# FoX attention on one core: splitting fp32 value products over two column tiles by query blocks instead of by even and odd key blocks

## The chip, the cores and the metric

The kernel runs on one core of a Trainium2 chip. The core has five engines with queues of their own: TensorE (PE), VectorE (DVE), ScalarE (ACT), GpSimd (POOL) and SyncE (SP), which issues most of the DMAs. The metric is the device time of one execution in microseconds. Of each kernel one further execution was profiled; all durations come from its trace.

## What is computed

One inference step of a small hybrid decoder: a recurrent layer (RG-LRU), then a forgetting-attention layer, for a prompt of 2048 tokens and for 8 sequences of 8 new tokens each that attend to 4096 cached tokens in pages. The change is in the attention of the prompt, which has 16 heads of 64 elements:

```python
def fox_block(q, k, v, cq, ck, q_pos, k_pos):
    s = jnp.einsum('bqhd,bkhd->bhqk', q, k).astype(jnp.float32) * (HEAD_DIM ** -0.5)
    s = s + jnp.swapaxes(cq, 1, 2)[:, :, :, None] - jnp.swapaxes(ck, 1, 2)[:, :, None, :]
    mask = k_pos[None, :] <= q_pos[:, None]
    s = jnp.where(mask[None, None], s, -jnp.inf)
    p = jax.nn.softmax(s, axis=-1)
    return jnp.einsum('bhqk,bkhd->bqhd', p.astype(v.dtype), v)
```

The last line is the value product: for each head, the weights `p` (keys by queries) times the values `v` (keys by 64). Everything is float32.

## The kernel before

**Stages.** The recurrent layer comes first, in two parts of the prompt; then the projections that make keys, values, queries and gates (`phase_b`, with streamed weights); then the prompt's attention (`attention`), and at the end the output projection (`project`). The decode of the 8 sequences (`decode`) reads 16 turns of cache pages by DMA, transposes the keys on DVE (`ktr`), makes scores on PE (`dS`) and value products on PE (`dO`). Two of its turns run earlier, the other fourteen beside the projections and the attention: `Side.along` takes steps of the decode in proportion to a cost that each step of the attention yields. The order of instructions on each engine is then set when the program is built, by a scheduler that works with a model of the engines; on the chip every engine runs its list in order.

**Units.** Attention works through 64 units, a head and a block of 512 queries each (`units`); even heads take the query blocks 0, 1, 2, 3 and odd heads 3, 2, 1, 0. A unit of query block `qc` has 4 x (`qc` + 1) blocks of 128 keys, so there are 640 key blocks in all. The last four key blocks of a unit are on the diagonal: the fourth sees only the last 128 queries, and `lo` is the first query that a key block needs (0, 128, 256, 384).

**One key block.** PE makes scores into an `st` bank (lines 1538 and 1539, on the diagonal also a causal mask, line 1541), ACT takes the exponential into `p` (line 1547), or into `acc` for the first key block of a unit. After every fourth key block a group of value products is recorded, to run two key blocks later (`product`). POOL then adds each `p` to `acc` (line 105, a helper), which gives the sums of the softmax. There are five `p` buffers and five `acc` buffers, two `st` banks, and one bank `ops` for the value products. Ahead of this, PE also makes the scores for the row maxima of later units (`sx`, line 1405), which DVE reduces.

**The value product.** The stationary operand is the values of 128 keys, 128 x 64; the moving operand is `p`, 128 x up to 512. An output has 64 rows, half of the array's columns. Even key blocks write rows 0 to 63 of `ops`, odd ones rows 64 to 127 (`r = k % 2 * HD`, line 1557), so two neighbouring products use two column tiles of the array. A group of four key blocks is held together in PE's order by `together`; it waits for the last of its four exponentials.

**The end of a unit** (`finish`). The two halves of `ops` are partial sums of the same output, over even and odd keys. ACT copies the upper rows to `oT` (line 1439) and the lower rows to `odd` (line 1443), and POOL adds `odd` to `oT` (line 105). Then come the sums' reduction (`total`), the normalisation (`norm`) and the gate, which reads `oT`.

The functions that the change touches:

Of the kernel before, what the change touches and what calls it, by code (L numbers as in the profile page):

```python
# [11 lines left out]
F32 = mybir.dt.float32  # L12
# [3 lines left out]
ALU = mybir.AluOpType  # L16
# [4 lines left out]
P = 128  # L21
# [7 lines left out]
HD = 64  # L29
# [15 lines left out]

SHARE = 1.13
LEAD = 18
ODD = "G"
RAMP = 8
NS = 3  # L50
SHARE0 = 2.0
# [33 lines left out]
def tile_hawk_fox(  # L85
# [8 lines left out]
    V, A, G, T, S = nc.vector, nc.scalar, nc.gpsimd, nc.tensor, nc.sync  # L94
# [9 lines left out]
    def tt(eng, out, a, b, op):  # L104
        eng.tensor_tensor(out, a, b, op=op)  # L105

    def together(mms, after=()):

        first = mms[0]().ins
        for d in after:  # L110
            tc.add_manual_dep(first, d.ins.name, SYNC)
        with tc.high_priority(), tc.issue_after(first):
            for mm in mms[1:]:
                mm()
# [91 lines left out]
    def sbuf(es, name, side=None):  # L206
        return es.enter_context(tc.tile_pool(name=name, bufs=1, side=side, reuse_waits="tile"))
# [1100 lines left out]
    def attention(es):  # L1308
        pool = sbuf(es, "att")
        ps3 = psum["att"]  # L1310

        ps3.tile([P, 512], F32, name="ops", tag="ops", bufs=1)
        ps3.tile([P, 512], F32, name="st", tag="st", bufs=2)
        pool.tile([P, 512], F32, name="acc", tag="acc", bufs=NACC)
        pool.tile([P, 512], F32, name="p", tag="p", bufs=NP)
# [3 lines left out]
        vvs = [pool.tile([P, 16, HD], F32, name=f"vvt{i}") for i in range(2)]  # L1319
# [38 lines left out]
        heads, qas, mxs, oTs_, sgt = {}, {}, {}, {}, {}  # L1358
# [10 lines left out]
        def load_keys(h):  # L1369
            kb = kbs[h % 2]  # L1370
            loaded.add(h)
            for lo, hi in halves(h):
                queue[0].dma_start(f(kb[0:64, lo:hi]), kd_d[h * HD:(h + 1) * HD, 1, lo:hi])
                queue[0].dma_start(f(kb[64:67, lo:hi]), nc_d[h, :, lo:hi])
# [14 lines left out]
        def load_low(u):  # L1389
            if u < len(units):  # L1390
                h, qc = units[u]
                qa = qas[u] = pool.tile([P, 512], F32R, name="qa", tag="qa", bufs=4)
                queue[0].dma_start(f(qa[:, :]), qd_d[h * HD:(h + 1) * HD, :, qc * 512:(qc + 1) * 512].rearrange("d x t -> (d x) t"))
# [36 lines left out]
        def finish(u, ops, acc):  # L1430
            h, qc = units[u]
            pr, h2 = divmod(h, 2)
            if u % 8 == 0:
                oTs_["sums"] = pool.tile([P, 32], F32, name="sums", tag="sums", bufs=2)
            sums = oTs_["sums"]
            if h2 == 0:
                oTs_[qc] = pool.tile([P, 512], F32, name="oT", tag="oT", bufs=5)
            oT = oTs_[qc][h2 * HD:(h2 + 1) * HD, :]
            A.copy(oT, ops[0:HD, :])
            lo = P if qc == 0 else 0  # L1440
            if ODD == "G":
                odd = pool.tile([P, 512], F32, name="odd", tag="odd")[h2 * HD:(h2 + 1) * HD, :]
                A.copy(odd[:, lo:], ops[HD:, lo:])
                tt(G, oT[:, lo:], oT[:, lo:], odd[:, lo:], ALU.add)
            else:
                tt(V, oT[:, lo:], oT[:, lo:], ops[HD:, lo:], ALU.add)
            accs.append((qc, acc))
            if len(accs) == 4 or h == H - 1:
                later.after(2, lambda todo=accs[:]: total(h2, sums, todo, h >= H - 2))
                accs.clear()  # L1450
            if u >= len(units) - 4:
                later.after(5, lambda oT=[oTs_[qc]]: norm(pr, sums, qc, 1, oT))
            elif u % 8 == 7:
                later.after(5, lambda oT=[oTs_[c] for c in range(4)]: norm(pr, sums, 0, 4, oT))
# [45 lines left out]
        start = [sum(nks[:u]) for u in range(len(units))]  # L1500
# [27 lines left out]
        ops = acc = None  # L1528
        pair = []
        for u, (h, qc) in enumerate(units):  # L1530
            load_low(u + 2)
            for k in range(nks[u]):
                ka, kb = heads[h], kbs[h % 2]
                qa, qb = qas[u], qbs[u % NQ]
                lo = max(0, k - qc * 4) * P
                ks = slice(k * P, (k + 1) * P)
                ps = ps3.tile([P, 512], F32, name="st", tag="st", bufs=2)
                T.matmul(ps[:, lo:], ka[:, ks], qa[:, lo:], start=True, stop=False)  # L1538
                T.matmul(ps[:, lo:], kb[:, ks], qb[:, lo:], start=False, stop=(k < qc * 4))  # L1539
                if k >= qc * 4:  # L1540
                    T.matmul(ps[:, lo:lo + P], identB[:, :], causal[:, :], start=False, stop=True)
                done[2] = u + (k == nks[u] - 1)
                if k == 0:
                    p = acc = pool.tile([P, 512], F32, name="acc", tag="acc", bufs=NACC)
                else:
                    p = pool.tile([P, 512], F32, name="p", tag="p", bufs=NP)
                pair.append((k, lo, p, A.activation(p[:, lo:], ps[:, lo:], AF.Exp)))  # L1547

                def product(u=u, h=h, todo=pair, acc=acc, last=(k == nks[u] - 1)):


                    nonlocal ops
                    if todo[0][0] == 0:
                        ops = ps3.tile([P, 512], F32, name="ops", tag="ops", bufs=1)

                    def mm(k, lo, p, _):
                        r = k % 2 * HD
                        return T.matmul(ops[r:r + HD, lo:], vvs[h % 2][:, k, :], p[:, lo:], start=(k < 2),  # L1558
                                        stop=(last and k >= todo[-1][0] - 1))

                    together([partial(mm, *x) for x in todo], [todo[-1][3]])
                    for k, lo, p, _ in todo:
                        if k:
                            tt(a_l(), acc[:, lo:], acc[:, lo:], p[:, lo:], ALU.add)
                    if last:
                        finish(u, ops, acc)

                if k % 4 == 3:
                    later.after(2, product)
                    pair = []  # L1570
                before = done[0]
                advance(tick)
                tick += 1
                later.tick()
                if k + sum(nks[u - u % 4:u]) == 0 and h + 1 < H:
                    load_keys(h + 1)
                if k + sum(nks[u - u % 4:u]) == 3 and h + 1 < H:
                    load_head(h + 1)
                yield 4.1 * (512 - lo) * 0.42 + (done[0] - before) * 213
# [130 lines left out]
    todo = a00.norm(2)  # L1710
# [35 lines left out]
    todo = a01.norm(3)  # L1746
# [40 lines left out]
    dec, att, last = ExitStack(), ExitStack(), ExitStack()  # L1787
# [11 lines left out]
    lin.close()  # L1799
    psum["att"] = banks(att, "psa", 6)  # L1800
    side.along(attention(att), share)
    side.upto(1e12)
    project(last)
# [37 lines left out]
```

## Time and profile before

| | |
|---|---|
| median of three runs | 3070.52 us (3066.45, 3070.52, 3083.66) |
| the profiled execution | 3073.57 us, span of its instructions 3071.8 us |
| busy over the span | PE 2826.8 us (92%), DVE 1805.2 (59%), ACT 1294.9 (42%), POOL 1158.7 (38%) |
| first and last value product | 1739.5 us, 2898.0 us |
| value products | 1152 records from `p` and 128 from `acc` |

A row of a group reads: line, engine, operation, output and inputs with their shapes, count; then total busy time in us and the mean of one in ns; then the idle time of that engine just before, and what ended it. A row of the timeline reads: start in us, duration in us, engine, line, operation, count; in brackets the idle time before it. A row of waits reads: who waited for whom, us in total, how often, the longest. A piece of the chain of work that ended last reads: start, duration, engine, tile and line. PE is the matmul, PEld the load of its stationary operand. An fp32 matmul of the program is two records in the trace. In a PE row, `128*64 128x512` is an operand of 128 rows for a tile of 64 columns, and 512 moving columns.

### The profile page before, as it was taken

To read this page: it belongs to the slowest core of one execution; us is meant where nothing else is said; L and a number is where in the kernel's file an instruction comes from. 1 tells how busy PE (TensorE), PEld (TensorE's weight loads), DVE (VectorE), ACT (ScalarE), POOL (GpSimd) and SP (SyncE) were. 2 spreads that over 40 slices of the span, in tenths; PEclk is the share of its full clock that TensorE was granted. 3 is DMA by queue.
4 is the path that set the end of the run, shared out by engine and by line. 5 is a ranking of instruction groups with operands and counts; after the bars stand their busy time and mean duration, and the time that the engine had idled before them with its cause. 6 is when DMAs were issued, how large, how long until landed. Compare 5 with 4: busy or idle time off the path is not lost.

```text
span 3071.8 us, 58144 instructions
## 1 busy us (share of the span) xinstructions
PE 2826.8 (92%) x20462; PEld 2178.9 (71%) x20462; DVE 1805.2 (59%) x4012; ACT 1294.9 (42%) x2874; POOL 1158.7 (38%) x1263
## 2 busy tenths in 40 slices
PE   5998999999999989997999798998989989999898
PEld 5997889988999978896888454555545554554587
DVE  7876555424357756755555566666667765543244
ACT  4665432222346655333333244343434445455321
POOL 1653201000025532000000365656565757788522
PEclk9999999999999999998999799999999999999999
DMA  4224547788622256999999998989999997322243
GB/s 121 91 76 147 157 137 209 239 256 260 209 82 86 86 180 202 318 312 313 329 311 316 303 285 258 293 276 306 294 309 316 328 286 236 107 67 68 83 143 111
DMA packets 492855, 653.25 MB, mean 213 GB/s; under 512 B 91100, under 2 KB 292829, under 8 KB 485286
## 3 DMA queue, kind: packets, MB, share of 16 engines
q1 hardware_dynamic: 488934, 643.87, 66.8%
q10 hardware_dynamic: 3340, 3.56, 0.4%
q8 instruction: 162, 2.65, 0.4%
q0 software_dynamic: 288, 2.10, 0.2%
q14 instruction: 131, 1.07, 0.1%
HBM read 513.82 MB, written 135.16 MB: 211 GB/s over the span
## 4 chain that ended last, share of the span: by engine, by line
PE 56%; DMA 18%; DVE 10%; ACT 6%; SPq 5%; issue 4%; POOL 2%; DVEq 0%; ACTq 0%; POOLq 0%
PE ops L1558 6%; DMA raw<-in_cache_k_dram 4%; PE y L367 4%; PE y L368 4%; PE y L369 4%; PE st L1538 4%; DMA raw<-in_cache_v_dram 4%; PE sx L1405 3%; PE kv L369 3%; PE kv L367 3%; PE kv L368 3%; PE dO L1236 3%; PE st L1539 3%; PE dS L1126 2%; PE qg L367 2%
## 5 line engine op out<-in xcount | busy, mean ns | idle before, releaser
L105 POOL TENSOR_TENSOR acc<-acc,p 128x512 f32<-128x512 f32 (+3 forms) x576 | 640.6, 1112 | 304.6 <-PE ops L1558 240.8
L1547 ACT ACTIVATE p<-st 128x512 f32<-128x512 f32 (+3 forms) x576 | 290.5, 525 | 409.5 <-PE st L1539 186.6
L1158 DVE STREAM_TRANSPOSE ktr<-raw 128x1024 f32<-128x1024 f32 x256 | 305.3, 1224 | 151.2 <-DMA raw<-in_cache_k_dram 141.8
L1407 DVE TENSOR_REDUCE mxs<-sx 128x1 f32<-128x512 f32 x384 | 253.6, 679 | 145.0 <-PE sx L1405 144.2
L368 PE MATMUL kv<-wl,xh 128*128 128x256 f32 (+3 forms) x1088 | 309.9, 288 | 9.0 <-DVE wl L412 8.8
L367 PE MATMUL kv<-wh,xh 128*128 128x256 f32 (+3 forms) x1088 | 311.0, 290 | 5.8 <-ACT wh L411 5.7
L369 PE MATMUL kv<-wh,xl 128*128 128x256 f32 (+3 forms) x1088 | 310.1, 287 | 0.0
L1558 PE MATMUL ops<-p,vvt 128*64 128x512 f32 (+3 forms) x1152 | 296.9, 554 | 2.3 <-ACT p L1547 2.1
L1538 PE MATMUL st<-qa,ka 128*128 128x512 f32 (+3 forms) x640 | 273.6, 428 | 21.1 <-ACT p L1547 16.6
L1405 PE MATMUL sx<-kbt,qbt 96*128 96x512 f32 (+3 forms) x640 | 232.3, 421 | 26.3 <-DMA qbt<-qd 10.6
L1538 PEld LDWEIGHTS st<-qa,ka 128*128 128x128 f32 x640 | 124.1, 194 | 179.5 <-issue 112.9
L411 ACT ACTIVATE wh<-wst,gv 128x256 fp32r<-128x256 f32 (+1 forms) x384 | 164.4, 499 | 187.7 <-DMA wst<-in_b_w_in_dram 73.2
L1539 PE MATMUL st<-qbt,kbt 128*128 128x512 f32 (+3 forms) x640 | 236.5, 371 | 0.0
L412 DVE SCALAR_TENSOR_TENSOR wl<-wst,gv,wh 128x256 fp32r<-128x256 f32 (+1 forms) x384 | 170.4, 494 | 104.6 <-ACT wh L411 100.8
L367 PE MATMUL qg<-xh,wh 128*128 128x384 f32 (+2 forms) x640 | 228.8, 359 | 0.0
L369 PE MATMUL qg<-xh,wl 128*128 128x384 f32 (+2 forms) x640 | 227.6, 357 | 1.1 <-DVE wl L412 1.0
L368 PE MATMUL qg<-xl,wh 128*128 128x512 f32 (+2 forms) x640 | 227.0, 356 | 0.0
L1091 POOL TENSOR_TENSOR qw<-qb,amask 128x128 f32<-128x128 f32 x64 | 29.8, 473 | 502.7 <-PE dS L1126 354.0
L368 PEld LDWEIGHTS kv<-wl,xh 128*128 128x128 f32 (+1 forms) x1088 | 204.3, 189 | 12.7 <-DVE wl L412 10.4
L367 PEld LDWEIGHTS kv<-wh,xh 128*128 128x128 f32 (+1 forms) x1088 | 204.3, 189 | 12.2 <-ACT wh L411 6.5
L369 PEld LDWEIGHTS kv<-wh,xl 128*128 128x128 f32 (+1 forms) x1088 | 206.0, 190 | 4.4 <-issue 4.3
L1405 PEld LDWEIGHTS sx<-kbt,qbt 96*128 96x128 f32 x640 | 117.6, 201 | 93.7 <-issue 31.1
(299 smaller groups left out, 6477.2 us busy)
## 6 DMA issues: line engine op xcount, KB each, us to landing
raw<-in_cache_k_dram SPq DMA_DIRECT2D x512, 256.0 KB
raw<-in_cache_v_dram SPq DMA_DIRECT2D x512, 256.0 KB
wst<-in_w_kv_dram SPq DMA_DIRECT2D x48, 512.0 KB
wst<-in_b_w_in_dram SPq DMA_DIRECT2D x48, 512.0 KB
xt<-in_x_prompt_dram SPq DMA_DIRECT2D x32, 512.0 KB
wst<-in_a_w_in_dram SPq DMA_DIRECT2D x64, 256.0 KB
out_dram<-kf SPq DMA_DIRECT2D x128, 128.0 KB
sc<-cd SPq DMA_DIRECT2D x16, 1024.0 KB
```

The costliest lines, as they stand in the source:

```text
L105: eng.tensor_tensor(out, a, b, op=op)
L367: T.matmul(ps, lh(k), rh(k), start=(k == 0), stop=False)
L368: T.matmul(ps, lh(k), rl(k), start=False, stop=False)
L369: T.matmul(ps, ll(k), rh(k), start=False, stop=(k == nk - 1))
L412: V.scalar_tensor_tensor(wl[:, k, :], st[:, k, :], gk, f(wh[:, k, :]), op0=ALU.mult, op1=ALU.subtract)
L1158: V.transpose(t.kts[pp][:, n], raw[:, :, pp * 256:(pp + 1) * 256])
L1405: T.matmul(ps[:, :w], qb[0:96, j * P:(j + 1) * P], kb[0:96, ck * 512:ck * 512 + w], start=True, stop=True)
L1407: V.reduce_max(mx[:, j, ck:ck + 1], ps[:, :w], axis=AX.X)
L1538: T.matmul(ps[:, lo:], ka[:, ks], qa[:, lo:], start=True, stop=False)
L1539: T.matmul(ps[:, lo:], kb[:, ks], qb[:, lo:], start=False, stop=(k < qc * 4))
L1547: pair.append((k, lo, p, A.activation(p[:, lo:], ps[:, lo:], AF.Exp)))
L1558: return T.matmul(ops[r:r + HD, lo:], vvs[h % 2][:, k, :], p[:, lo:], start=(k < 2), stop=(last and k >= todo[-1][0] - 1))
```

## The change

Each key block now has two value products instead of one, with the same stationary operand: query blocks 0 and 2 of the unit go to the first column tile, query blocks 1 and 3 to the second (`r` = 0, 1). Each product is at most 256 wide and reads `p` with a step. The output of a unit is then 128 x 256, complete in both halves, and takes half a bank; units take the two halves of one bank in turn. At a unit's end ACT makes two copies of 64 x 256 straight into the places of `oT`; `odd` and POOL's add are gone. A diagonal key block has products only where a query block needs it: a group on the diagonal has seven products, a full group eight, where both had four.

```diff
-ODD = "G"
...
-        ps3.tile([P, 512], F32, name="ops", tag="ops", bufs=1)
+        ops2 = ps3.tile([P, 512], F32, name="ops", tag="ops", bufs=1)
...
-            oT = oTs_[qc][h2 * HD:(h2 + 1) * HD, :]
-            A.copy(oT, ops[0:HD, :])
-            lo = P if qc == 0 else 0
-            if ODD == "G":
-                odd = pool.tile([P, 512], F32, name="odd", tag="odd")[h2 * HD:(h2 + 1) * HD, :]
-                A.copy(odd[:, lo:], ops[HD:, lo:])
-                tt(G, oT[:, lo:], oT[:, lo:], odd[:, lo:], ALU.add)
-            else:
-                tt(V, oT[:, lo:], oT[:, lo:], ops[HD:, lo:], ALU.add)
+            oT = oTs_[qc][h2 * HD:(h2 + 1) * HD, :].rearrange("d (a r c) -> d a r c", a=2, r=2)
+            for r in range(2):
+                A.copy(oT[:, :, r, :], ops[r * HD:(r + 1) * HD, :].rearrange("d (a c) -> d a c", a=2))
...
                     if todo[0][0] == 0:
-                        ops = ps3.tile([P, 512], F32, name="ops", tag="ops", bufs=1)
-
-                    def mm(k, lo, p, _):
-                        r = k % 2 * HD
-                        return T.matmul(ops[r:r + HD, lo:], vvs[h % 2][:, k, :], p[:, lo:], start=(k < 2),
-                                        stop=(last and k >= todo[-1][0] - 1))
-
-                    together([partial(mm, *x) for x in todo], [todo[-1][3]])
+                        ops = ops2[:, u % 2 * 256:u % 2 * 256 + 256]
+
+                    def mm(k, lo, p, r):
+                        a0 = (lo // P + 1 - r) // 2
+                        return T.matmul(ops[r * HD:(r + 1) * HD, a0 * P:], vvs[h % 2][:, k, :],
+                                        p[:, :].rearrange("p (a r c) -> p a r c", a=2, r=2)[:, a0:, r, :],
+                                        start=(k == 0), stop=(last and k == todo[-1][0] - 1 + r))
+
+                    together([partial(mm, k, lo, p, r) for k, lo, p, _ in todo for r in range(2) if lo <= (2 + r) * P],
+                             [todo[-1][3]])
```

Up to the first value product the order of instructions is the same on every engine. From there on it differs, since the scheduler places the new instructions. In the changed kernel lines up to 1308 are numbered one lower, and the products have line 1551 instead of 1558. On PE, at the first two groups of value products (the diagonal of unit 0, then the first group of unit 1), before:

```order
8757 L1558 MATMUL ops<-acc,vvt_19534 64x512
8758 L1558 MATMUL ops<-p,vvt_19534 64x384
8759 L1558 MATMUL ops<-p,vvt_19534 64x256
8760 L1558 MATMUL ops<-p,vvt_19534 64x128
8761 L1538 MATMUL st<-qa,ka 128x512
...
8773 L1541 MATMUL st<-causal,identB 128x128
8774 L1558 MATMUL ops<-acc,vvt_19534 64x512
8775 L1558 MATMUL ops<-p,vvt_19534 64x512 x3
```

And in the changed kernel, where `x6` counts equal neighbours:

```order
8757 L1551 MATMUL ops<-acc,vvt_19534 64x256 x2
8758 L1551 MATMUL ops<-p,vvt_19534 64x128
8759 L1551 MATMUL ops<-p,vvt_19534 64x256
8760 L1551 MATMUL ops<-p,vvt_19534 64x128 x3
8761 L1531 MATMUL st<-qa,ka 128x512
...
8773 L1404 MATMUL sx<-kbt_19537,qbt_19541 128x512 x2
8774 L1551 MATMUL ops<-acc,vvt_19534 64x256 x2
8775 L1551 MATMUL ops<-p,vvt_19534 64x256 x6
```

The diagonal group went from four products to seven and the full one from four to eight, at the same places. On POOL, from the sums of unit 0 to those of unit 2 (`qw` and `gmx` belong to the decode), before:

```order
461 L105 TENSOR_TENSOR acc<-acc,p 128x384
462 L105 TENSOR_TENSOR acc<-acc,p 128x256
463 L105 TENSOR_TENSOR oT<-oT,odd 64x384
464 L105 TENSOR_TENSOR acc<-acc,p 128x128
465 L105 TENSOR_TENSOR acc<-acc,p 128x512 x3
466 L1091 TENSOR_TENSOR qw<-qb,amask 128x128
467 L105 TENSOR_TENSOR acc<-acc,p 128x512
```

And in the changed kernel:

```order
461 L104 TENSOR_TENSOR acc<-acc,p 128x384
462 L104 TENSOR_TENSOR acc<-acc,p 128x256
463 L104 TENSOR_TENSOR acc<-acc,p 128x128
464 L104 TENSOR_TENSOR acc<-acc,p 128x512 x4
465 L1090 TENSOR_TENSOR qw<-qb,amask 128x128 x2
```

The add of `odd` stood in front of an add to `acc` and is gone. On PE, where the decode's key scores (`dS`) stand beside the first groups of the fourth unit, before:

```order
8872 L1558 MATMUL ops<-acc,vvt_19534 64x512
8873 L1558 MATMUL ops<-p,vvt_19534 64x512 x3
8874 L1538 MATMUL st<-qa,ka 128x512
8875 L1539 MATMUL st<-qbt_19541,kbt_19537 128x512
8876 L1126 MATMUL dS<-ktr,qw 32x128 x32
8877 L1405 MATMUL sx<-kbt_19545,qbt_19542 128x512 x3
...
8885 L1558 MATMUL ops<-p,vvt_19534 64x512 x4
```

And in the changed kernel:

```order
8871 L1551 MATMUL ops<-acc,vvt_19534 64x256 x2
8872 L1551 MATMUL ops<-p,vvt_19534 64x256 x6
8873 L1531 MATMUL st<-qa,ka 128x512
8874 L1532 MATMUL st<-qbt_19541,kbt_19537 128x512
8875 L1203 MATMUL dsum<-ddg,ones 128x64
...
8884 L1551 MATMUL ops<-p,vvt_19534 64x256 x8
...
8898 L1125 MATMUL dS<-ktr,qw 32x128 x32
```

One group of key scores now stands behind the second group of value products of this unit instead of behind the first; by the 240th key block both orders have issued 1536 of these matmuls.

## The prediction

> **What bounds the kernel now.** The order of instructions is the same in both kernels until the first value product of the prompt's attention, so I first read the busy time of each engine in the three stretches that can differ: attention beside the decode, attention after the decode has ended, and the output projection.
>
> ```profile
> span 3071.8 us, 58144 instructions
> core 0: us, PE busy (x) PEld busy (x) DVE busy (x) ACT busy (x) POOL busy (x), PEclk, DMA share, GB/s
> 1740.00:2580.00 840.00, 775.10 (x6778) 441.13 (x6775) 565.12 (x1156) 371.04 (x900) 524.50 (x505) 0.96 0.94 295
> 2580.00:2898.00 318.00, 293.41 (x1265) 156.73 (x1264) 136.45 (x318) 162.50 (x340) 242.25 (x210) 0.97 0.33 88
> 2898.00:3072.00 174.00, 158.98 (x678) 127.95 (x676) 76.00 (x243) 33.98 (x77) 44.58 (x36) 0.96 0.39 127
> ```
>
> For 840 us two resources are full together: PE is busy for 92% of the time and the DMA engines for 94%, on the cache pages of the decode. In the next 318 us only PE is full (293.4 us, 24.6 us idle); POOL is at 76% and ACT at 51%. The last stretch holds no value product but the end of the very last one, and I leave it as it is. Next, the chain of work that ended last, by line, in the first and in the second stretch:
>
> ```profile
> by line: PE ops L1558 14.8%; PE st L1538 8.9%; PE sx L1405 7.3%; DMA raw<-in_cache_v_dram 7.3%; PE dO L1236 7.3%; DMA raw<-in_cache_k_dram 6.9%; PE st L1539 6.0%; PE dS L1126 5.8%; issue 4.4%; SPq L1073 3.7%; DMA rawn<-ksd 2.5%; DVE ktr L11
> by line: PE ops L1558 22.9%; PE st L1538 12.4%; PE sx L1405 8.6%; PE st L1539 8.2%; issue 4.0%; ACT p L1547 3.8%; PE y L367 3.6%; PE y L369 3.5%; PE y L368 3.5%; PE tot L1461 3.4%; DMA wst<-in_b_w_out_dram 3.1%; DMA ogd<-sgt 2.3%; SPq L466
> ```
>
> The value products themselves (`ops`) are the largest item of both: 14.8% of 840 us and 22.9% of 318 us, 124 + 73 = 197 us. So two questions decide: does a value product get dearer on PE, and how much of what ACT and POOL are spared stands on the chain?
>
> **PE: twice the products at half the width.** This is one group of four key blocks in the trace of before, in time order (start, duration, engine), with the first load of what follows it; then a diagonal group, and two groups of the decode that use narrower column tiles, and the loads of both kinds over the whole run:
>
> ```profile
> 2408.80 0.20 PEld L1558 LDWEIGHTS ops<-p,vvt 128*64 128x64 f32 x4 [0.36 <-ACT p L1547]
> 2408.81 1.94 PE L1558 MATMUL ops<-p,vvt 128*64 128x512 f32 x8
> 2409.29 0.14 PEld L1558 LDWEIGHTS ops<-p,vvt 128*64 128x64 f32 x2 [0.29 <-issue]
> 2409.72 0.14 PEld L1558 LDWEIGHTS ops<-p,vvt 128*64 128x64 f32 x2 [0.29 <-issue]
> ...
> 2420.29 1.50 PE L1558 MATMUL ops<-p,vvt 128*64 128x512 f32 x8
> ...
> 2405.43 1.07 PE L1236 MATMUL dO<-raw,sx 128*32 128x256 f32 x16
> ...
> 2422.73 1.96 PE L1126 MATMUL dS<-ktr,qw 128*32 128x128 f32 x64
> ...
> L1558 PEld LDWEIGHTS ops<-p,vvt x1152: 132/137/232, 1739.5 to 2897.8; 128*64 128x64 f32 x192
> ...
> L1126 PEld LDWEIGHTS dS<-ktr,qw x4096: 106/110/178, 579.4 to 2508.7; 128*32 128x32 f32 x196
> ```
>
> Each fp32 product is two records, so four products are eight. The loads of a pair come 0.43 us apart (2409.29, 2409.72): two records, one in each column tile, run side by side. Per tile the full group is four records of 512 columns, the `dO` group (four column tiles) four of 256, and the `dS` group sixteen of 128. With a start a, a charge c per record and s per column: a + 4c + 1024s = 1.07, a + 4c + 2048s = 1.94, a + 16c + 2048s = 1.96. The first two give s = 0.85 ns a column, the last two 12c = 0.02 us, c = 1.7 ns. So sixteen narrow records cost what four wide ones do.
>
> After the change a full group has, per tile, eight records of 256 columns: the same 2048 columns, four more charges, 1.94 + 0.007 us. In a diagonal group the longer tile had 2 x (512 + 256) = 1536 columns (even blocks) and then has 2 x (256 + 256 + 128 + 128) = 1536 (odd query blocks): also only four charges. There are 640 / 4 = 160 groups, so PE gains 160 x 0.007 = 1.1 us of work; the chain carried 197 us of the (96 x 1.94 + 64 x 1.50) = 282 us that these groups take, 70%, so +0.8 us. From below: nothing makes the streaming shorter, so no gain; from above, the second and third rival.
>
> The Trainium skill speaks against the change here: "TensorEngine Tiling (Array Packing)", section Instruction Overhead, gives each matmul about 60 cycles of overhead; at the 2.4 GHz of "TensorE: Matmul & The Clock Gate" that is, as an estimate, 25 ns, so four more records in each of 160 groups would cost 16 us of PE and the sum below would end some 11 us later. The `dS` row does not agree: at 25 ns its twelve additional records a tile would show 0.3 us, and it shows 0.02.
>
> **ACT and POOL at the end of a unit.** Here are the copies and the add that the change replaces, the two rows nearest to the new copy (256 elements a partition), and what was waited for:
>
> ```profile
> L1439 ACT COPY oT<-ops 64x512 f32<-64x512 f32 x64 | 37.1, 579 | 107.4 <-PE ops L1558 107.3
> L1443 ACT COPY odd<-ops 64x512 f32<-64x512 f32 (+1 forms) x64 | 35.6, 556 | 0.9
> L105 POOL TENSOR_TENSOR oT<-oT,odd 64x512 f32<-64x512 f32 (+1 forms) x64 | 77.3, 1208 | 88.2 <-ACT odd L1443 85.2 <-issue 2.3
> L1547 ACT ACTIVATE p<-st 128x256 f32<-128x256 f32 x63 | 24.0, 381 | 23.0 <-PE st L1541 13.9 <-POOL acc L105 8.5
> L1260 ACT COPY ob<-dO 128x256 f32<-128x256 f32 x11 | 4.1, 371 | 17.1 <-PE dO L1244 17.0
> ACT p L1547 <- POOL acc L105: 34.9, 34, 3.6
> ACT p L1547 <- POOL acc L105: 17.9, 18, 3.4
> ```
>
> Two copies of 0.579 and 0.556 become two of about 0.375 (the copy's own row says 371, the exponential's 381): 0.385 us a unit, 64 x 0.385 = 24.6 us of ACT. POOL loses 64 adds, 77.3 us, and the wait in front of them (85.2 us for the `odd` copy) in which later `acc` adds stood behind it in POOL's queue. Those adds free the five `p` buffers, and ACT waited for them 34.9 us in all, 17.9 of it in the second stretch. Little of this is on the chain, though. It has 7 pieces of the first copy (7 x 0.58), 8 of the second (2.86 us in all, five of them near full length), 3 of the add and 7 of `acc` adds (5.4 us in all); first and last of each, and all of the add:
>
> ```profile
> 1866.36 0.58 ACT oT L1439
> 1866.95 0.59 ACT odd L1443
> 1884.66 1.28 POOL oT L105
> 1893.01 1.01 POOL oT L105
> ...
> 1891.11 1.02 POOL acc L105
> ...
> 2820.45 0.58 ACT oT L1439
> 2821.04 0.59 ACT odd L1443
> 2821.70 1.27 POOL oT L105
> 2822.97 0.42 POOL acc L105
> ```
>
> First copies: 7 x 0.205 = -1.4 us. The five long second copies: 2.70 - 5 x 0.375 = -0.8. The add: -3.6. Of the `acc` pieces five stand right behind an add of `oT` (3.7 us); half of that, -1.8, because the product they wait for is late next. With PE's +0.8 the sum is -6.8 us. Ends: 0 if PE or a cache page is late at the same moment anyway, and the whole idle time of PE in the second stretch, 24.6 us, as the first rival has it.
>
> What costs nothing. The half banks: the first product of the next unit starts behind its own four exponentials, and ACT, in order, has made the copies before those in both kernels, so the single bank was no wait and two halves free none. The last unit's shorter end lies beside the projection. `odd` leaves SBUF, which nothing asks for. SP's own instructions are unchanged; their places move a little (fourth rival).
>
> The profiled execution took 3073.57 us (span 3071.8), 3.05 over the median of 3070.52. Against its own time the sum gives 3066.8, against the median 3063.7: **3064 us**.
>
> **Rivals.**
>
> 1. *The queues drain better than the chain shows*: 3047 us. The chain names only the last of several late things. In the second stretch nothing but PE is full; ACT's 17.9 us behind POOL and 19 units x 0.385 = 7.3 us of copies add up to 25.2, just what would fill PE's 24.6 us of idle time. 3070.5 - 24.6 + 0.8. For it: POOL at 76% there, with units whose adds come in runs. Against: much of that idle time is the turn-round from score to exponential to product.
>
> 2. *A charge for every record*: 3082 us. The first two records of a group that I looked at stand 0.48 us apart from their successors and the later ones 0.43 to 0.44:
>
> ```profile
> 2402.90 0.64 PE L1558 MATMUL ops<-acc,vvt 128*64 128x512 f32 x1
> ...
> 2403.38 0.59 PE L1558 MATMUL ops<-acc,vvt 128*64 128x512 f32 x1
> ```
>
> If that 0.04 us were due for each record and not once a group: 4 x 160 x 0.04 x 0.70 = 18 us on 3064. At the price that the Trainium skill gives under Instruction Overhead it would be 3075. Against both: the `dS` row.
>
> 3. *Loads no longer hidden*: 3121 us, the slower side. A load of 64 columns takes 137 ns; a record of 256 columns streams for 0.218 us, so the two tiles' loads hide only while they overlap. Taken in turn they need 0.274: +0.056 x 8 = 0.45 us in a full group, and in a diagonal one 14 x 0.137 - 1.31 = 0.61. 96 x 0.45 + 64 x 0.61 = 82 us, 70% on the chain, 57. It decides once a load in turn exceeds 0.109 us. For it: loads double. Against: `dS` hides four loads of 110 ns behind every 0.11 us.
>
> 4. *The decode moves*: 3086 us. PE's order places a group of key scores later near the fourth unit. There are 38 of them (x2432 records of 64) in the first stretch, one each 22 us; if the pages behind it come one group late and the DMA engines, 94% full, never make it up, +22 us.
>
> ```profile
> L1126 PE MATMUL dS<-ktr,qw 128*32 128x128 f32 x2432 | 80.1, 287 | 5.5 <-DVE ktr L1158 3.4 <-issue 1.0 <-DVE oTs L105 0.9
> ```
>
> Against: 6% of 840 us is 50 us of slack, and by mid-stretch the decode stands level in both orders.
>
> **How the numbers follow.** Forecast 0.50; rivals 0.22, 0.08, 0.07, 0.13. Three runs of before lie 17 us apart, and a difference of about 0.5% (15 us) is what a measurement can tell from none: faster means under 3055, slower over 3086. Faster: 0.20 of the first rival and 0.09 of the forecast's lower part, 0.29. Slower: the third rival 0.07, half the fourth 0.07, and 0.05 of the others' upper parts, 0.19. The same: 0.52. The range is 3040 to 3092: below it 0.06 of the first rival, above it the third (0.07) and 0.05 of the fourth.
>
> **What would show it.** Right: a full group of sixteen `ops` records still takes 1.9 to 2.0 us, the copies 0.37 to 0.38 us, POOL is some 77 us less busy, ACT's wait for `acc` adds is shorter than 34.9 us, and the first stretch is as long as before. Wrong: full groups of 2.1 us or more (rivals 2 and 3, told apart by gaps that equal a load), `dO` products waiting longer for cache pages (rival 4), or a second stretch shorter by 20 us (rival 1).

## The result and the profile after

The changed kernel takes 3055.42 us, the median of five runs (3054.65 to 3064.68); the kernel before took 3074.63 beside it (five runs, 3066.45 to 3083.66). The ratio is 0.9945, with an interval of [0.9926, 0.9964]. A second set of runs (`n2_after_again`, below) gives 0.9959 [0.9940, 0.9978]. By the medians the change saves 19 and 14 us, by the ratios 0.55% and 0.41% (17 and 13 us); against the twelve runs of `n1_before_again`, the same kernel as before, the second set is 10 us lower. Forecast were 6.8.

From the page of the changed kernel, whose profiled execution took 3055.27 us: the span, busy time of the engines, and the value products with their loads.

```profile
span 3053.6 us, 60463 instructions
PE 2827.0 (93%) x21614; PEld 2258.5 (74%) x21614; DVE 1810.2 (59%) x4012; ACT 1269.8 (42%) x2874; POOL 1079.6 (35%) x1199
L1551 PE MATMUL ops<-p,vvt 128*64 128x256 f32 (+1 forms) x2176 | 261.0, 366 | 3.4 <-ACT p L1540 2.8
L1551 PEld LDWEIGHTS ops<-p,vvt 128*64 128x64 f32 x2176 | 161.2, 140 | 92.6 <-issue 22.7
```

PE has 1152 more records and is as busy as before (2827.0 against 2826.8). ACT lost 25.1 us of work (1294.9 to 1269.8; forecast 24.6), POOL 79.1 (1158.7 to 1079.6; forecast 77). A full group of value products in the timeline (start, duration):

```profile
2702.48 0.65 PE L1551 MATMUL ops<-acc,vvt 128*64 128x256 f32 x4
2702.97 1.47 PE L1551 MATMUL ops<-p,vvt 128*64 128x256 f32 x12
```

It runs from 2702.48 to 2704.44: sixteen records in 1.96 us, where eight took 1.94. From the first record of a group to the first of what follows, the median over the run is 1.88 us for a full group (before 1.87) and 1.45 for one on the diagonal (before 1.43). The new copies, and ACT's wait for the `acc` adds:

```profile
L1439 ACT COPY oT<-ops 64x256 f32<-64x256 f32 x128 | 46.9, 367 | 109.2 <-PE ops L1551 105.3 <-POOL acc L104 2.8
ACT p L1540 <- POOL acc L104: 29.1, 24, 2.8
```

A copy takes 0.367 us (forecast 0.375). The wait is 29.1 us over the run, where it was 34.9.

To place the gain, I cut the attention at two marks that all kernels have: the copy that ends unit 1 and that which ends unit 43 (units are counted from 1 here, so unit 1 is the unit 0 of the lists of orders). The last 21 units, up to the copy that ends unit 64, lie almost wholly behind the decode, whose last `dO` product comes 19 to 24 us after the second mark. Each pair of rows has units 2 to 43 and then 44 to 64; the columns are those of the table of windows in the prediction. Before, and the kernel before run again:

```profile
1741.89:2549.09 807.20, 742.60 (x6540) 424.29 (x6541) 549.91 (x1123) 357.89 (x873) 500.65 (x484) 0.96 0.95 297
2549.09:2899.10 350.01, 324.38 (x1495) 172.64 (x1495) 151.36 (x347) 176.47 (x368) 266.74 (x232) 0.98 0.36 101
```
```profile
1732.23:2545.22 812.99, 740.73 (x6540) 420.15 (x6541) 545.90 (x1126) 357.93 (x873) 500.19 (x484) 0.96 0.94 294
2545.22:2897.52 352.30, 326.44 (x1495) 174.00 (x1495) 151.69 (x347) 176.47 (x368) 266.39 (x232) 0.97 0.36 101
```

The changed kernel, and the changed kernel run again:

```profile
1732.57:2541.19 808.62, 744.84 (x7320) 473.42 (x7320) 545.93 (x1121) 341.29 (x872) 451.74 (x444) 0.96 0.95 296
2541.19:2881.24 340.05, 322.21 (x1861) 199.41 (x1861) 159.45 (x354) 167.85 (x369) 238.32 (x208) 0.98 0.36 103
```
```profile
1733.84:2548.53 814.69, 749.59 (x7320) 475.37 (x7321) 542.50 (x1117) 341.31 (x873) 451.06 (x443) 0.95 0.94 293
2548.53:2886.26 337.73, 319.95 (x1861) 198.21 (x1861) 158.32 (x354) 167.90 (x370) 239.22 (x208) 0.99 0.36 103
```

Beside the decode nothing changed: 807.2 and 813.0 us before, 808.6 and 814.7 after. The last 21 units went from 350.0 and 352.3 to 340.0 and 337.7, on average 12.3 us less. PE's idle time there (stretch less busy time) fell from 25.6 and 25.9 to 17.8 and 17.8, which is 8 of the 12.3; the busy time fell by the other 4.3. The start of the first row, 1741.9 against 1732.6, is no part of it, as the second rows show: the kernel before has 1732.2 there when it runs again.

The busy time holds the effect of the clock. Cut into windows of 5 us, the time lost to it (one minus the granted clock, times the length, summed) is 8.5 and 12.0 us before and 5.1 and 1.7 after. This is a matter of the last 21 units alone: in units 2 to 43 the loss is 34.0 and 30.7 us before and 35.8 and 41.1 after, so over all of them it is 42.5 and 42.7 before and 40.9 and 42.8 after. What such a loss is shows in the trace of before, in windows of 1 us, with the granted clock third from the right:

```profile
2741.00:2742.00 1.00, 0.82 (x7) 0.49 (x6) 0.00 (x0) 0.83 (x3) 1.00 (x1) 1.00 0.00 0
2742.00:2743.00 1.00, 0.70 (x2) 0.26 (x2) 0.00 (x0) 1.00 (x4) 0.92 (x2) 1.00 0.16 49
2743.00:2744.00 1.00, 0.28 (x1) 0.28 (x2) 0.00 (x0) 0.81 (x3) 0.92 (x2) 1.00 0.82 166
2744.00:2745.00 1.00, 1.00 (x6) 0.41 (x7) 0.00 (x0) 0.45 (x1) 0.92 (x2) 0.86 0.61 197
2745.00:2746.00 1.00, 1.00 (x7) 0.61 (x4) 0.00 (x0) 0.14 (x1) 0.92 (x2) 0.50 0.02 6
2746.00:2747.00 1.00, 1.00 (x5) 0.24 (x2) 0.00 (x0) 0.04 (x1) 0.60 (x1) 0.50 0.00 0
2747.00:2748.00 1.00, 1.00 (x3) 0.81 (x4) 0.00 (x0) 0.99 (x2) 0.00 (x0) 0.50 0.00 0
2748.00:2749.00 1.00, 1.00 (x6) 0.75 (x4) 0.58 (x1) 0.73 (x2) 0.72 (x1) 0.94 0.00 0
```
```profile
2743.72 0.50 PE L1538 MATMUL st<-qa,ka 128*128 128x512 f32 x1 [1.02 <-ACT acc L1547]
2744.38 2.53 PE L1558 MATMUL ops<-p,vvt 128*64 128x512 f32 x8
```

PE is busy for 0.82, 0.70 and 0.28 of three microseconds (the last with 1.02 us of waiting for ACT), and then the clock stands at half for about 3.4 us. The group of value products in it takes 2.53 us. The losses of the windows add up to 0.14 + 3 x 0.50 + 0.06 = 1.7 us: a stall of 1.2 us can be paid again, and more, after it has ended. It need not be. When the kernel before ran again, the same wait of 1.02 us stood at the same place, the clock stayed at full speed, and the same group took 1.50 us:

```profile
2741.00:2742.00 1.00, 0.72 (x2) 0.28 (x2) 0.00 (x0) 1.00 (x4) 0.92 (x2) 1.00 0.19 53
2742.00:2743.00 1.00, 0.26 (x1) 0.26 (x2) 0.00 (x0) 0.83 (x3) 0.92 (x2) 1.00 0.80 156
2743.00:2744.00 1.00, 1.00 (x6) 0.45 (x7) 0.00 (x0) 0.43 (x1) 0.92 (x2) 1.00 0.59 199
```
```profile
2743.41 1.50 PE L1558 MATMUL ops<-p,vvt 128*64 128x512 f32 x8
```

So the length of a stall alone does not decide whether the clock falls; no run here shows what else does. In units 44 to 64 the clock goes down five times in each of the two traces of before, and three times and once in those of the changed kernel.

### The profile page after: what moved, and what is told of

Its sections match the earlier page's. It is cut to its first block, busy times and chain, and to the rows that moved or that the text cites. A ratio compares the mean times of both kernels' runs of the same rounds, so it can differ in the third digit from the quotient of the medians.

```text
span 3053.6 us, 60463 instructions
## 1 busy us (share of the span) xinstructions
PE 2827.0 (93%) x21614; PEld 2258.5 (74%) x21614; DVE 1810.2 (59%) x4012; ACT 1269.8 (42%) x2874; POOL 1079.6 (35%) x1199
## 3 DMA queue, kind: packets, MB, share of 16 engines
q14 instruction: 131, 1.07, 0.1%
## 4 chain that ended last, share of the span: by engine, by line
PE 59%; DMA 18%; DVE 9%; ACT 5%; SPq 4%; issue 3%; POOL 2%; DVEq 0%; ACTq 0%; POOLq 0%
PE ops L1551 6%; PE y L368 4%; PE y L366 4%; PE y L367 4%; DMA raw<-in_cache_v_dram 4%; PE kv L366 4%; PE kv L367 4%; PE kv L368 4%; DMA raw<-in_cache_k_dram 4%; PE st L1531 3%; PE sx L1404 3%; PE dO L1235 3%; PE dS L1125 2%; PE st L1532 2%; PE qg L366 2%
## 5 line engine op out<-in xcount | busy, mean ns | idle before, releaser
L1531 PE MATMUL st<-qa,ka 128*128 128x512 f32 (+3 forms) x640 | 273.9, 428 | 12.2 <-ACT p L1540 11.0
L1551 PE MATMUL ops<-p,vvt 128*64 128x256 f32 (+1 forms) x2176 | 261.0, 366 | 3.4 <-ACT p L1540 2.8
L1551 PEld LDWEIGHTS ops<-p,vvt 128*64 128x64 f32 x2176 | 161.2, 140 | 92.6 <-issue 22.7
```

Of the source, the lines that this page charges most:

```text
L1551: return T.matmul(ops[r * HD:(r + 1) * HD, a0 * P:], vvs[h % 2][:, k, :], p[:, :].rearrange("p (a r c) -> p a r c", a=2, r=2)[:, a0:, r, : ...
```

## The experiments

My theory was that POOL's queue made the difference: without the add of `odd`, the `acc` adds come sooner. The rivals were ACT's shorter copies, and the mere order of instructions, which the scheduler chooses anew for each kernel. Below, "idle" and "clock" are PE's idle time and the time lost to the clock in units 44 to 64. The comparison in each case is the kernel before on the same chip (medians 3074.68 to 3075.32).

| run | median us | ratio | units 2 to 43 | units 44 to 64 | idle | clock |
|---|---|---|---|---|---|---|
| n1_before_again | 3071.01 | 0.9985 [0.9968, 1.0003] | 813.0 | 352.3 | 25.9 | 12.0 |
| n2_after_again | 3060.67 | 0.9959 [0.9940, 0.9978] | 814.7 | 337.7 | 17.8 | 1.7 |
| x1_key_new_end | 3074.63 | 1.0001 [0.9980, 1.0021] | 826.0 | 345.4 | 23.1 | 8.5 |
| x3_query_pool_add | 3070.14 | 0.9985 [0.9971, 1.0000] | 815.6 | 349.7 | 24.3 | 5.1 |
| o1_before_share | 3096.52 | 1.0066 [1.0053, 1.0080] | 837.8 | 347.3 | 25.7 | 10.2 |
| v1_before_dve | 3078.18 | 1.0008 [0.9996, 1.0021] | 834.1 | 340.3 | 23.2 | 6.8 |
| b1_after_dve_copy | 3080.39 | 1.0010 [0.9998, 1.0021] | 827.7 | 335.0 | 22.2 | 3.4 |
| b2_after_six_p | 3062.75 | 0.9953 [0.9940, 0.9966] | 809.2 | 343.9 | 22.7 | 11.9 |
| s1_key_seq | 3135.85 | 1.0204 [1.0156, 1.0252] | 899.5 | 326.4 | 24.4 | 6.8 |
| s2_query_seq | 3092.26 | 1.0067 [1.0039, 1.0095] | 869.0 | 311.1 | 14.0 | 0.0 |
| s3_query_pool_seq | 3099.03 | 1.0086 [1.0053, 1.0119] | 870.0 | 320.3 | 16.8 | 3.4 |
| s4_key_new_end_seq | 3108.04 | 1.0132 [1.0089, 1.0176] | 881.8 | 316.0 | 19.2 | 1.7 |

The stage columns come from one profiled execution each; those of `b1` and `b2` are 10 and 12 us shorter than their medians, those of `v1`, `x1` and `x3` are 6, 4 and 4 longer. The last 21 units also hold unequal work: the order decides how many of the decode's last `dO` products lie behind the second mark. There are 128 PE records of them before and in `n1`, 96 in the changed kernel, `n2` and `x3`, 80 in `x1`, 64 in `b2`, 48 in `v1`, 32 in `o1` and `b1`, and none in the four `s` runs; a group of 16 takes 1.07 us, so up to 6 us between two kernels of that column is work that stands elsewhere. Between the kernel before and the changed one it evens out, as an estimate: two groups of `dO` fewer (2.1 us), five records of `sx` and two of `st` more (about 0.3 us each by the spacing of such records in the trace of before).

**Both kernels again.** No edit.

> The kernel before once more, unchanged, for the spread from run to run. In its first profile the copy that ends unit 1 began at 1741.9 us, in that of the changed kernel at 1732.6, though up to the first value product both run the same instructions in the same order. Theory (the 9 us in front of the attention are spread from run to run): here it lies anywhere between 1730 and 1745. Rival (they belong to the program): 1741 to 1743. Both expect a ratio of 1.000 and some 297 us from the copy that ends unit 45 to the one that ends unit 64.

> The changed kernel once more. Theory (spread): the end of unit 1 lies anywhere between 1730 and 1745. Rival (program): 1732 to 1734. Both expect a ratio of 0.993 to 0.996, 860 us from the end of unit 1 to that of unit 45 as before the change, and some 288 us from there to the end of unit 64.

Units 44 to 64 repeat within 2.3 us in each kernel, units 2 to 43 only within about 6. The start of the attention moved by 9.7 us between two executions of the kernel before. So the gain stands, and it lies in the last 21 units.

**One part at a time.** `x1` keeps the products over even and odd keys and has the new end of a unit; half of each partial sum is left out:

```diff
-            oT = oTs_[qc][h2 * HD:(h2 + 1) * HD, :]
-            A.copy(oT, ops[0:HD, :])
...
-                A.copy(odd[:, lo:], ops[HD:, lo:])
-                tt(G, oT[:, lo:], oT[:, lo:], odd[:, lo:], ALU.add)
...
+            oT = oTs_[qc][h2 * HD:(h2 + 1) * HD, :].rearrange("d (a r c) -> d a r c", a=2, r=2)
+            for r in range(2):
+                A.copy(oT[:, :, r, :], ops[r * HD:(r + 1) * HD, :].rearrange("d (a r c) -> d a r c", a=2, r=2)[:, :, r, :])
```

> Products by even and odd key blocks as before, four in a group, but the new end of a unit: two copies of 64x256, no odd copy and no add on POOL. It leaves out half of each partial sum (of every second query block the even keys, of the others the odd keys). Theory (the gain of the second stretch comes from the end of a unit): units 45 to 64 take 286 to 291 us as in the changed kernel, ratio 0.993 to 0.998. Rival (it comes from the narrower products, which release acc and p for POOL's adds earlier): 295 to 298 us, ratio 0.998 to 1.001.

`x3` is the changed kernel with an add on POOL put back at the end of a unit:

```diff
+            odd = pool.tile([P, 512], F32, name="odd", tag="odd")[h2 * HD:(h2 + 1) * HD, :]
...
-                A.copy(oT[:, :, r, :], ops[r * HD:(r + 1) * HD, :].rearrange("d (a c) -> d a c", a=2))
+                A.mul(odd[:, r * 256:(r + 1) * 256], ops[r * HD:(r + 1) * HD, :], 0.5)
+            x0 = odd.rearrange("d (r a c) -> d a r c", r=2, a=2)
+            tt(G, oT, x0, x0, ALU.add)
```

> The changed kernel with an add on POOL put back: the two short copies go to odd (halved), and POOL adds odd to itself into oT, 64x512, some 1.28 us for each unit. Theory (POOL's add and the queue behind it carry most of it: 3.6 + 1.8 of the 7.6 us worked out on the chain): units 45 to 64 take 292 to 296 us, ratio 0.996 to 0.999. Rival (the shorter copies on ACT carry it): 287 to 290 us, ratio 0.993 to 0.996.

In units 44 to 64, `x3` stands at 349.7, 10 to 12 us above the changed kernel and level with the one before: for the theory, at first sight. `x1` gains only 5 to 7 us there, and its whole time gains nothing, since its units 2 to 43 are 13 to 19 us longer than before: against the theory. `x1` only takes work away from ACT and POOL, so order was tried next.

`x3` holds more than that. By the traces, PE issues the same records in the same order in `x3` and in the changed kernel from the start up to the end of unit 48 (but for one pair that swaps places within 0.01 us), so up to there POOL's add is tested with PE's order held fixed. Over units 2 to 43 it costs nothing clear of the spread: 815.6 us against 808.6 and 814.7. From the second mark to the last record before the orders part, in the changed kernel, in `n2` and in `x3`:

```profile
2541.19:2646.63 105.44, 97.97 (x604) 59.55 (x604) 64.29 (x135) 51.66 (x113) 67.87 (x55) 0.97 0.51 154
2548.53:2652.45 103.92, 96.70 (x604) 59.01 (x604) 63.74 (x135) 51.73 (x113) 68.74 (x55) 0.98 0.51 156
2549.35:2657.56 108.21, 97.95 (x604) 59.73 (x604) 65.06 (x135) 51.85 (x113) 73.81 (x60) 0.97 0.49 150
```

Here the add costs 2.8 to 4.3 us over five units, and nearly all of PE's additional idle time is a wait for DVE's row maxima (`sx` behind `mxs`: 3.7 us against 1.0 and 1.2), not for exponentials. The other 7 to 8 of the 10 to 12 us come after the orders have parted.

**Order alone.** The same instructions as before; a constant that says how much of the decode is recorded beside each piece of the other work is 1% lower, and PE's order differs from 1416 us on, before the attention starts:

```diff
-SHARE = 1.13
+SHARE = 1.12
```

> The kernel before with SHARE at 1.12 for 1.13: the same instructions at the same cost, placed differently by the scheduler (some steps of the decode move by a key block or two). It measures what the order alone does. From the end of unit 43 to that of unit 64 before took 350.1 and 352.3 us, the changed kernel 340.0 and 337.7. Theory (that gain is cost taken away, not order): 347 to 354 us, with 23 to 28 us of PE idle. Rival (order alone moves as much): outside that, by 5 us or more.

The time rises by 0.66% [0.53, 0.80], 20 us, as much as the change under study moves it, or more. The two stretches, with units 2 to 43 first:

```profile
1736.45:2574.23 837.78, 753.44 (x6628) 427.40 (x6629) 542.93 (x1117) 358.40 (x873) 500.89 (x486) 0.94 0.93 289
2574.23:2921.58 347.35, 321.66 (x1407) 171.63 (x1407) 156.22 (x353) 175.99 (x370) 265.18 (x229) 0.97 0.34 93
```

The loss is in the stretch beside the decode: 837.8 us, with 88 more PE records in it than before, PE idle for 84.3 (64.6 and 72.3 in the two profiles of before) and 51.1 us lost to the clock (34.0 and 30.7). In units 44 to 64 idle time and clock loss are those of before, 25.7 and 10.2, as the theory of this run had it. So a ratio of the whole time can't tell the parts of this change apart, while the waits in the last 21 units can still be read.

**The add on DVE.** DVE adds the lower rows of `ops` straight to `oT`; no `odd`, no add on POOL, but the copy of 64 x 512 stays on ACT.

```diff
-ODD = "G"
+ODD = "V"
```

> The kernel before with its other branch: DVE adds the odd half straight from the bank, with no odd copy and no add on POOL. Products by even and odd key blocks stay. Theory (half of the gain is the end of a unit, half the narrower products, as x1's 345.4 and s4 say): unit 43 to 64 takes 343 to 347 us, ratio 0.995 to 1.000. Rival (the end of a unit is all): 337 to 341 us, ratio 0.993 to 0.997; or DVE's add, behind the row maxima in its queue, holds the bank: 350 us or more.

**The second copy on DVE.** The changed kernel, with one of its two copies moved from ACT to DVE.

```diff
-                A.copy(oT[:, :, r, :], ops[r * HD:(r + 1) * HD, :].rearrange("d (a c) -> d a c", a=2))
+                cp((A, V)[r], oT[:, :, r, :], ops[r * HD:(r + 1) * HD, :].rearrange("d (a c) -> d a c", a=2))
```

> The changed kernel with the second of the two copies on DVE instead of ACT. Theory (POOL's queue and the stalls of PE carry the gain, ACT's copies little): unit 43 to 64 takes 337 to 341 us, as in the changed kernel. Rival (ACT's copies delay the exponentials behind them): 331 to 336 us.

**Six `p` buffers.** The changed kernel with one buffer more, so that ACT waits less for POOL.

```diff
-NP = 5
+NP = 6
```

> The changed kernel with six p buffers for five, in the room that odd left. Theory (exponentials wait for buffers that POOL's adds hold, 12 to 18 us from unit 43 to 64, and PE behind them): that wait falls under 6 us, PE's idle time there from 17.8 to 10 to 15 us, and the stretch takes 331 to 336 us, ratio to before 0.990 to 0.994. Rival (PE's idle time is the turn-round through two st banks): 337 to 341 us.

`v1` and `b1` are shorter than before in units 44 to 64 (340.3 and 335.0, as the rivals of both runs had it for this stretch, though not the ratio in `v1`), in part because 80 and 96 fewer `dO` records stand there; they are longer beside the decode, and no gain remains. In `b2` ACT's wait for `acc` adds in units 44 to 64 is 8.9 us (12.0 and 18.1 in the changed kernel's two profiles), not under 6 as expected. It buys nothing: the interval lies within that of the changed kernel's second runs, and PE's idle time is 22.7 us where it was 17.8. So nothing shows that PE's time hung on that wait. None of these beats the changed kernel.

What PE waited for is in its own waits. In units 44 to 64 its waits for ACT fall from 18.1 and 18.5 us to 10.3 and 10.1, which is all of the 8 us of idle time. The rows of units 44 to 64 that name ACT's exponentials (total, times, longest); of before:

```profile
PE st L1538 <- ACT p L1547: 9.0, 17, 1.7
PE ops L1558 <- ACT p L1547: 5.4, 6, 2.3
PE st L1538 <- ACT acc L1547: 2.9, 4, 1.0
```

Of the changed kernel (no row for `acc`):

```profile
PE st L1531 <- ACT p L1540: 7.5, 14, 1.2
PE ops L1551 <- ACT p L1540: 2.8, 5, 1.1
```

Of `v1`, with the long copy and no add on POOL, and of `x3`, with short copies and the add:

```profile
PE st L1538 <- ACT p L1547: 9.9, 15, 3.8
PE st L1538 <- ACT acc L1547: 2.3, 4, 0.7
PE ops L1558 <- ACT p L1547: 1.9, 5, 0.9
```
```profile
PE ops L1554 <- ACT p L1543: 6.2, 5, 3.3
PE st L1534 <- ACT p L1543: 4.9, 12, 1.0
PE st L1534 <- ACT acc L1543: 0.7, 1, 0.7
```

Scores that wait for ACT to empty a bank (`st`, both rows together) cost 11.9 us before, 11.8 in `n1`, 11.6 in `o1` and 12.2 in `v1`, all with a copy of 512. They cost 7.5 in the changed kernel, 6.9 in `n2`, 6.0 in `x1`, 5.6 in `x3`, 8.0 in `b1` and 6.4 in `b2`, all with short copies. That gap alone does not make the copies the cause: `s1` below, with the long copies, has 8.6, and 3.8 of the 12.2 us of `v1` are one wait in which ACT first stands idle and then casts weights of the output projection:

```profile
2609.82 2.24 ACT L98 CAST woh<-wst 128x1024 fp32r<-128x1024 f32 x2 [4.69 <-issue]
2611.96 1.08 ACT L1547 ACTIVATE p<-st 128x512 f32<-128x512 f32 x2
2612.60 0.79 PE L1538 MATMUL st<-qa,ka 128*128 128x512 f32 x1 [3.82 <-ACT p L1547]
```

A stricter count follows each of PE's waits for ACT to the instruction that ended it, and ACT's queue back from there as long as ACT does not pause for more than 0.15 us, and asks whether a copy of a unit's end lies in that run. One such wait, of before:

```profile
2841.66 0.58 ACT L1439 COPY oT<-ops 64x512 f32<-64x512 f32 x1 [0.79 <-PE ops L1558]
2842.25 0.58 ACT L1443 COPY odd<-ops 64x512 f32<-64x512 f32 x1
2842.86 1.09 ACT L1547 ACTIVATE p<-st 128x512 f32<-128x512 f32 x2
2843.51 0.51 PE L1538 MATMUL st<-qa,ka 128*128 128x512 f32 x1 [0.79 <-ACT p L1547]
```

In units 44 to 64 such waits add up to 5.0 us before, 5.2 in `n1`, 4.5 in `o1` and 5.7 in `s1`, all with two long copies; to 1.5 in `v1`, with one; to 1.0 in the changed kernel and in `n2`, 2.1 in `x1`, 1.4 in `x3`, 1.1 in `b2`, and 1.0, 1.2 and 3.3 in `s2`, `s3` and `s4`, with two short ones; and to none in `b1`, with one short copy. They go with ACT's copies through every order and with or without POOL's add. So some 4 of the 8 us of idle time belong to ACT's shorter copies, against my theory; the other 4 us are waits for ACT with no copy in front of them, and their cause stays open. The value products' wait for exponentials (`ops`) is 5.4 and 5.9 before and 2.8 twice after; but it is 6.2 in `x3`, 8.1 in `x1` and 1.9 in `v1`, and that order fits neither POOL's add nor the copies alone.

**With the decode recorded first.** To take the interleaving out, four of the kernels were recorded with the decode kept whole ahead of the attention:

```diff
-    def beside():
-        yield from decode(dec, turns[FIRST:], 4, 2, True)
-        dec.close()
-        yield from project_ready(last)
-
-    side = Side(beside())
+    side = Side(decode(dec, turns[FIRST:], 4, 2, True))
...
     side.along(gen, share)
+    side.upto(1e12)
+    dec.close()
+    side = Side(project_ready(last))
```

> The kernel before with the decode run to its end ahead of the attention, so that no cache page is fetched beside a value product; all 64 units then stand in a stretch like the last third of before, which only PE fills. It is the reference for the next three. All theories expect that the whole gets longer (the decode is no longer hidden) and that the stretch from the end of unit 1 to that of unit 64 is far shorter than the 1157 us of before: 204 of 640 key blocks took 297 us, so about 930 us less what the output projection's rows took there.

> The changed kernel in the same form. Theory (the end of a unit delays PE by 0.45 to 0.6 us, 8.6 to 10.9 us over 19 units, and the cache pages hide that in the other 45): unit 1 to unit 64 takes 28 to 36 us less than in s1. Rival (the 9 to 11 us belong to the order of the last third, not to each unit): less than 12 us.

> The same with the short copies and an add of 64x512 on POOL put back at the end of each unit. Theory (POOL's queue carries the gain): within 8 us of s1. Rival (the copies on ACT carry it): within 8 us of s2.

> Products by even and odd key blocks, with the short copies and no add (half of each partial sum is left out), in the same form. Theory (the end of a unit is all of it): within 8 us of s2. Rival (it is one part beside the narrower products, as the 5.4 us of 8.6 to 10.9 in the last third of x1 suggest): 10 to 20 us under s1.

This missed its aim. The scheduler put the two side by side again: the last `dO` product of `s1` comes at 2544.5 us, and units 2 to 43 grew to 899.5 us. Nor did the expected distances come out: `s3` lies 36.8 us below `s1`, where the theory wanted the two level; it is within 6.8 us of `s2`, as the rival (the copies) had it. `s4`, with the new end of a unit alone, lies 27.8 below `s1` and 15.8 above `s2`, where neither side had it. The short copies are in both `s3` and `s4`, so the two distances are not parts of the 43.6 us from `s1` to `s2`. PE's order is the same in `s2` and `s3` up to 2586.2 and 2589.1 us, but for neighbours that swap: from the first mark to there they take 850.2 and 851.2 us, so POOL's add again costs nothing that shows beside the decode. In units 44 to 64, with no `dO` product left in them, idle and clock together are 31.2 (`s1`), 20.2 (`s3`), 20.9 (`s4`) and 14.0 (`s2`), and of the 15.3 us from `s1` to `s2` the new end alone (`s4`) has 10.4, with an order of its own.

## Why the prediction was right, and where its sum was off

The measured 3055.42 us lies 9 us under the forecast and 8 above the first rival's 3047, in a range 52 us wide: the time alone does not choose between the two, and that the range held says little about the sum. What can be judged is each step.

- **Wider or narrower products cost PE the same: right.** Forecast 1.94 + 0.007 us for a full group; the timeline has 1.96, the medians 1.87 and 1.88. Rivals 2 and 3 needed 2.1 us or more. The price under Instruction Overhead in "TensorEngine Tiling (Array Packing)" of the Trainium skill would be, as an estimate, 0.1 us for the four more records of a tile; the medians differ by a tenth of that, so the trace does not agree. Loads doubled and stayed hidden (PE's busy time is unchanged).
- **The stretch beside the decode as long as before: right, but its reason was not.** I took the DMA engines, at 94%, for its limit, with 50 us of slack behind it. `o1` has the DMA engines at 93% and needs 25 to 31 us more than before, with PE idle for 84.3 us and busy for 11 to 13 us more. So the order of instructions can move this stretch by more than the whole forecast, and 94% was no sign that it would not. That it stayed as long here was in part luck; rival 4 had priced a move of this kind, but in the changed kernel it did not fall due (`PE dO` waits for value pages 23.5 us against 18.9 before, but 25.7 when the kernel before ran again).
- **The copies, -1.4 and -0.8: mis-sized.** The step read them off the chain of waits, where only the last of several late things has a piece. PE's waits behind such a copy fell from 5.0 and 5.2 us to 1.0 in the last 21 units alone, half of the 21 x 0.385 = 8.1 us that ACT was spared there; the forecast had 2.2 for the whole run. The rival that said so (1) had the mechanism, but it took all of PE's idle time for gain and a stretch 20 us shorter; 8 of 26 us of idle time went, and the last 21 units are 12.3 us shorter.
- **POOL's add, -3.6, and the `acc` adds behind it, -1.8: not shown.** ACT's wait for `acc` adds fell from 34.9 to 29.1 us in the first pair of profiles, but the second executions have 27.9 before and 29.8 after, so that sign was no evidence. Putting the add back cost 10 to 12 us in units 44 to 64 (`x3`), but only 2.8 to 4.3 of it while PE's order was the same, and there PE waited for DVE, not for exponentials behind `acc` adds; how much of the rest is order stays open.
- **Left out of the sum: the clock.** In the last 21 units it lost 8.5 and 12.0 us before, 5.1 and 1.7 after: 6.9 us less on the average, as much as the whole forecast, though two profiles of one kernel differ by half of that and over units 2 to 64 the loss is nearly unchanged. I priced each stall at its length. Here a stall of one to two microseconds brought 1.7 more when the clock fell, and none when it did not. "TensorE: Matmul & The Clock Gate" of the Trainium skill, Part 1, has the clock fall to half after an idle window of about 3.4 us and come back after a busy one of that length. The trace agrees in that the half clock lasted 3.4 us; but it followed 1.2 us of idle time spread over three microseconds in which PE also worked.

Together, units 44 to 64: PE's idle time -8.0 us and its busy time -4.3, -12.3; the forecast had -6.8 for the run. The clock's -6.9 is a part of the busy time and not a third term. Without it the busy time would have grown by some 2.5 us, as an estimate; of that the groups of value products have 33 x 0.01 + 21 x 0.02 = 0.8 us by their medians, and the rest is open. The direction and the range held; the size of the gain did not. About 4 us of it are shown to be ACT's shorter copies. How the rest divides between POOL's add, the clock and the order of the products is not settled: beyond the part of `x3` that ran in the changed kernel's order, every edit also changed the order.

## What to carry to other kernels

Where one engine is the bound and idles in small pieces, add up its own waits by the engine that it waits for; the chain of waits prices only what came last, and a stall on the matmul engine is to be priced with the half clock that may follow it. To tie such a wait to one operation, follow it back along the queue of the engine that ended it. Splitting a matmul of 512 columns into two of 256 was free here, where each column tile streams the same number of columns and the loads stay hidden. Where a scheduler sets the order, run a variant with the same instructions in another order before a difference below 1% is put down to one part of a change: here that alone moved the time by 0.66%. Compare the order of two traces, too: as long as it is the same, a difference in time belongs to the edit or to the spread.

## What was not expected of the hardware

- The granted clock stood at half for about 3.4 us after PE had been idle for only 1.2 us of the three microseconds ahead (windows 2741 to 2749 of before), and lost about 1.7 us; after the same wait of 1.02 us in `n1_before_again` it did not fall.
- How long the stretch beside the decode takes is not told by the DMA engines' load: units 2 to 43 took 807 and 813 us before at 95% and 94% of it, and 838 us in another order of the same program at 93%.
